# The norm's factor taken out of the opening's products: squares from x's own layout, products from a transposed x, a rescale at the end of the gates

## The chip, the cores and the metric

The kernel runs on one core of a Trainium2 chip. The metric is the time of one execution on the device in microseconds. Its engines are TensorE (PE, with its weight loads PEld), VectorE (DVE), ScalarE (ACT), GpSimd (POOL) and SyncE (SP), and each works through a queue of its own in order. Transfers are issued from the queues of SP, ACT and POOL.

## What is computed

One encoder layer for 512 tokens of width 2048, in float32. What matters here is its first step, a norm, and the projection behind it, of which the opening and the gates compute a part:

```python
def rmsnorm(x, w):
    y = x * lax.rsqrt(jnp.mean(x * x, axis=-1, keepdims=True) + EPS)
    return y * w

h = rmsnorm(x, norm_w)
u = h @ w_in        # columns: z_ssm, xbc, dt_f, dt_b, q_a, kv_a, z_attn, g_ssm, g_attn
xbc = silu(dwconv(xbc, conv_w, conv_b))          # along the tokens, 4 taps
dtf = softplus(dt_f + dt_bias_fwd)               # and dtb
y = ssd_scan(xs, dtf, ...) + flip(ssd_scan(...))
y = rmsnorm_groups(y * silu(z_ssm))
merged = sigmoid(g_ssm) * (y @ w_proj_ssm) + sigmoid(g_attn) * (o @ w_proj_attn)
return rmsnorm(x + merged @ w_out, final_norm_w)
```

The norm's factor is one number for each token, rsqrt(mean(x^2) + EPS), and h @ w_in is linear in it: it can be applied to h or to the product's rows.

## The kernel before

Every product in float32 is made of three products of rounded parts: a value is split into a high part (ScalarE casts) and the rest (VectorE subtracts), and high x high, high x low and low x high are added up in PSUM. `wchunk` (line 157) loads a chunk of 512 KB of a weight into `wraw`, casts it to `wh` and subtracts to `wl`, with three buffers for each; `mm3` (line 167) makes the three products. A tile of the projection has 16 such steps on 128 output columns and 512 tokens, from two chunks.

The opening (lines 195 to 241): x comes in eight transfers of 512 KB on SP's queue, in the layout tokens x width. ScalarE squares and sums each piece (line 210), `small_rsqrt` (lines 182 to 192) makes the factor of 128 tokens, VectorE and ScalarE scale x by it (lines 218 and 220), TensorE transposes it in 64 pieces (`x_turn`, line 225), and `x_out` (lines 227 to 230) makes h_h and h_l, the two parts of the transposed h, times the norm's weight. Then come the products: the tile of dt (`dtp`), and five tiles of xbc in the order 4, 5, 0, 1, 2, with a sixth, 3, after them. Each xbc tile goes through `conv_silu` (lines 384 to 393): a first step on ScalarE, three on VectorE, a SiLU on ScalarE, and is put to DRAM. After the second and the fourth of them `h_sums` (lines 706 to 731) makes, on half the width each, the sums that the Strassen products of the gates need: S1, S2 and S4 are split and kept, S3 and x21 are put to DRAM. `dt_make` (lines 278 to 303) turns dtp into dt and its decay in some twenty steps of VectorE, among the last xbc tiles.

Then the gates (lines 783 to 788): three weights of 2048 x 2048 (wz, wgs, wga), each in two pairs of columns by Strassen's scheme, a pair of seven products P1, P5, P6, P2, P3, P7 and P4 (`pair`, from line 642; `product`, line 545). A product has 48 steps of 128x512 and takes four chunks. X and Y are four buffers each: X is loaded for P1, then GpSimd adds the neighbouring block to it by a transfer that accumulates (`w_more`, line 497, issue on line 500), P5 takes that, VectorE adds Y for P6, and so on. In the first pair S3 is loaded back over a part of h_h (`h_part`), in the last pair of wga x21 (`h_back`). X, Y and the sums' buffers (pool `wx`) lie where the pool `sx` of the opening lay, and a buffer's first load waits for what last used the place. At a pair's end an activation (SiLU or sigmoid) is applied and the gate is put to DRAM. After the gates the state-space part begins: `dt_turn` (line 305) transposes dt, BT and CT and four xs are loaded from what the opening put (lines 897 to 901).

What sets the order: TensorE's order is the one in which the code is written. The other engines' instructions are ordered by a scheduler with priorities; `high_priority` with AHEAD = 60 or LOAD_AHEAD = 160 draws loads and splits forward.

## Time and profile before

| | us |
|---|---|
| time, median of 3 runs | 2056.31 (2055.39 to 2057.18) |
| the profiled execution | 2057.74 |
| its span, first to last instruction | 2055.9 |
| TensorE busy | 1967.2 (96%) |
| VectorE busy | 1463.4 (71%) |
| ScalarE busy | 968.9 (47%) |
| GpSimd busy | 317.7 (15%) |
| mean granted clock of TensorE | 0.986 |

The busy shares are means over the whole execution. The change touches the first 140 us, the last pair of wga and the head of the state-space part (from 571 us), so the timeline and windows of those places tell more than the page's shares. In a timeline a row is one instruction or a run of like ones, with what ended the idle time before it in brackets.

### The profile page before, as it was taken

Reading aid. Unit: us, or ns where it says so; the run is one execution under the profiler, and the core shown is the slowest. Engines: PE = TensorE matmul, PEld = TensorE weight load, DVE = VectorE, ACT = ScalarE, POOL = GpSimd, SP = SyncE. Lnnn points to the kernel's source line nnn. Section 1 sums busy time; section 2 is a strip of 40 time slices with the busy share of each in tenths; the row PEclk is TensorE's granted clock in tenths of the full one; section 3 lists DMA queues with packets and bytes.
Section 4 is the critical chain, followed back from the end, with each engine's and each line's share of the span. In section 5 each row is a group of like instructions: output and inputs, shape, how many; then the busy total and the mean of one; then the engine's idle time right before and its main releaser. Section 6 shows DMA issues by size and latency. Waiting matters only on the chain.

```text
span 2055.9 us, 24708 instructions
## 1 busy us (share of the span) xinstructions
PE 1967.2 (96%) x9074; PEld 1623.9 (79%) x9074; DVE 1463.4 (71%) x1946; ACT 968.9 (47%) x1352; POOL 317.7 (15%) x337
## 2 busy tenths in 40 slices
PE   6999999999989999998999989999999999999998
PEld 5878888888868787777788878888877777888886
DVE  7976676676659789799686567667675888776342
ACT  6444445444445656546545344444354454443232
POOL 0001011010033152332321101210010211100120
PEclk9999999999999999999999999999999999999999
DMA  5468657657446757687464857883386876865332
GB/s 196 164 179 202 171 126 195 184 120 188 134 169 188 220 149 209 201 231 220 150 194 149 232 164 185 221 209 88 83 212 246 302 256 260 273 219 169 108 118 82
DMA packets 166584, 378.56 MB, mean 184 GB/s; under 512 B 16000, under 2 KB 65280, under 8 KB 165888
## 3 DMA queue, kind: packets, MB, share of 16 engines
q1 hardware_dynamic: 104688, 238.33, 35.4%
q0 software_dynamic: 26944, 92.29, 20.5%
q10 hardware_dynamic: 34832, 46.38, 6.3%
q8 instruction: 71, 1.16, 0.2%
q14 instruction: 49, 0.40, 0.1%
HBM read 325.03 MB, written 98.04 MB: 206 GB/s over the span
## 4 chain that ended last, share of the span: by engine, by line
PE 72%; DVE 13%; DMA 7%; issue 4%; ACT 3%; SPq 0%; ACTq 0%; POOL 0%; DVEq 0%; POOLq 0%
PE P L564 10%; PE P L565 10%; PE P L563 10%; PE f L1497 3%; PE f L1498 3%; PE f L1496 3%; PE xbc L168 2%; PE xbc L169 2%; PE xbc L170 2%; PE za L168 2%; PE za L169 2%; DVE sum L1002 2%; PE za L170 2%; DVE wl L164 2%; DVE wl L434 1%
## 5 line engine op out<-in xcount | busy, mean ns | idle before, releaser
L434 DVE TENSOR_TENSOR wl<-X,wh 128x1024 fp32r<-128x1024 f32 x152 | 185.4, 1223 | 86.7 <-ACT wh L433 86.1
L164 DVE TENSOR_TENSOR wl<-wraw,wh 128x1024 fp32r<-128x1024 f32 (+2 forms) x148 | 171.9, 1162 | 89.7 <-ACT wh L163 89.4
L433 ACT CAST wh<-X 128x1024 fp32r<-128x1024 f32 x152 | 159.5, 1053 | 160.0 <-PE P L565 139.1
L163 ACT CAST wh<-wraw 128x1024 fp32r<-128x1024 f32 (+2 forms) x150 | 145.0, 969 | 147.5 <-PE za L169 41.9
L434 DVE TENSOR_TENSOR wl<-wraw,wh 128x1024 fp32r<-128x1024 f32 x74 | 91.4, 1235 | 97.5 <-ACT wh L433 97.4
L168 PE MATMUL xbc<-h_h,wh 128*128 128x512 f32 x384 | 151.9, 396 | 0.0
L170 PE MATMUL xbc<-h_h,wl 128*128 128x512 f32 x384 | 150.2, 391 | 0.9 <-DVE wl L164 0.9
L169 PE MATMUL xbc<-h_l,wh 128*128 128x512 f32 x384 | 149.9, 390 | 0.0
L563 PE MATMUL P<-wh,h_h 128*128 128x512 f32 x384 | 149.4, 389 | 0.0
L564 PE MATMUL P<-wl,h_h 128*128 128x512 f32 x384 | 149.4, 389 | 0.0
L565 PE MATMUL P<-wh,h_l 128*128 128x512 f32 x384 | 149.4, 389 | 0.0
L434 DVE TENSOR_TENSOR wl<-Y,wh 128x1024 fp32r<-128x1024 f32 x80 | 97.9, 1224 | 72.0 <-ACT wh L433 71.9
L433 ACT CAST wh<-wraw 128x1024 fp32r<-128x1024 f32 x74 | 78.0, 1054 | 144.7 <-PE f L1498 69.7
L433 ACT CAST wh<-Y 128x1024 fp32r<-128x1024 f32 x80 | 84.2, 1054 | 110.4 <-PE P L565 100.5
L564 PE MATMUL P<-wl,S 128*128 128x512 f32 x288 | 112.4, 390 | 0.8 <-DVE wl L434 0.8
L563 PE MATMUL P<-wh,S 128*128 128x512 f32 x288 | 112.1, 389 | 0.0
L565 PE MATMUL P<-wh,S 128*128 128x512 f32 x288 | 112.1, 389 | 0.0
L168 PE MATMUL za<-h_h,wh 128*128 128x512 f32 x256 | 101.7, 397 | 0.0
L170 PE MATMUL za<-h_h,wl 128*128 128x512 f32 x256 | 100.2, 391 | 1.0 <-DVE wl L164 1.0
L169 PE MATMUL za<-h_l,wh 128*128 128x512 f32 x256 | 100.0, 391 | 0.0
L1002 DVE TENSOR_TENSOR_SCAN sum<-da,scn 128x512 f32<-128x512 f32 x64 | 90.0, 1422 | 0.0
L170 PEld LDWEIGHTS xbc<-h_h,wl 128*128 128x128 f32 x384 | 72.4, 188 | 16.8 <-DVE wl L164 1.4
(634 smaller groups left out, 5184.6 us busy)
## 6 DMA issues: line engine op xcount, KB each, us to landing
wraw<-wi SPq DMA_DIRECT2D x102, 512.0 KB, 3.9
T_wps<-wps POOLq DMA_DIRECT2D x32, 512.0 KB, 6.0
da<-da_d SPq DMA_DIRECT2D x64, 256.0 KB, 4.5
T_wpa<-wpa POOLq DMA_DIRECT2D x32, 512.0 KB, 9.1
wraw<-wo SPq DMA_DIRECT2D x32, 512.0 KB, 3.4
wraw<-wps SPq DMA_DIRECT2D x24, 512.0 KB, 4.8
xbc_d<-xbc ACTq DMA_DIRECT2D x24, 256.0 KB, 3.7
wraw<-wun SPq DMA_DIRECT2D x16, 384.0 KB, 3.1
```

The lines of the kernel that those rows point to most:

```text
L163: act.copy(h, raw)
L164: (dve if ahead[0] else pool).tensor_sub(l, raw, h.bitcast(F32))
L168: pe.matmul(out, wh, xh, start=start, stop=False)
L169: pe.matmul(out, wh, xl, start=False, stop=False)
L170: pe.matmul(out, wl, xh, start=False, stop=stop)
L433: act.copy(hi_, raw)
L434: dve.tensor_sub(lo_, raw, hi_.bitcast(F32))
L563: pe.matmul(bs[i], xh, wh, start=(j == 0), stop=False)
L564: pe.matmul(bs[i], xh, wl, start=False, stop=False)
L565: pe.matmul(bs[i], xl, wh, start=False, stop=(j == 7))
L1002: dve.tensor_tensor_scan(sums[dd], flat(da), mask, 0.0, ALU.add, ALU.mult)
L1496: pe.matmul(acc, mh, wh, start=(start and k == 0), stop=False)
```

## The change

The host gives x a second time, transposed (`xt`), in pieces that lie as h_h does. h_h and h_l are made from it and the norm's weight, without the token's factor: no transposes, no scaling of x. The first three tiles (xbc 4, 5 and 0) are interleaved in the order "AAAABBBB AABB AABB C x 8, A x 8, B x 8, C x 8" as x's pieces land; two products on a constant stand ahead of them. x in its own layout is loaded after that, for the squares alone, through three buffers. `token_factors` makes the factor of all tokens at once, and `factor`, in TensorE's order at step 12 of the fourth xbc tile, spreads it to R (512 tokens in every partition) with four products; R is put to DRAM.

`xbc_done` multiplies a tile by R on VectorE ahead of its convolution, through one buffer `v_x`, for all six tiles. x_t is scaled by the norm's weight in place (16 operations of VectorE) and put to DRAM in eight pieces. `h_sums` takes x_t itself, so the eight additions of h_h and h_l go. dtp is the last tile; it is put to DRAM as it is, and `dt_make` runs in the first pair of wz, behind P5, from what it loads back, times R. The gates' activation takes the factor as its scale. In the last pair of wga, x11, x12, x21 and x22 are loaded back (eight transfers, before two), multiplied by R on VectorE and split over h_h and h_l, so that what comes after the gates has the norm's whole h. Lines of the Strassen class and of the head of wps are written differently with the same instructions.

The core of the diff:

```diff
-    act.dma_start(cst, a["cst"])
-    act.dma_start(vec, a["vec"])
+    act.dma_start(vec, a["vec"])
+    act.dma_start(cst, a["cst"])
...
+    warm_ps = pc("warm")
+    dve.memset(v_x, 1.0)
+    for _ in range(2):
+        pe.matmul(warm_ps, v_x[:, 0:P], v_x, start=True, stop=True)
+    ahead[0] = 1
+    firsts_i = (T_XBC + 4, T_XBC + 5, T_XBC)
+    early = [[] for _ in firsts_i]
+    for j in range(8):
+        for n, at in ((0, 0), (1, 2), (2, 4), (0, 4), (1, 6)):
+            if at == j:
+                early[n].append(wchunk(a["wi"][firsts_i[n], len(early[n])], 1024))
+        xs = x_t[:, 2 * j:2 * j + 2, :].rearrange("p k t -> p (k t)")
+        nc.sync.dma_start(xs, a["xt"][j])
+        for k in (2 * j, 2 * j + 1):
+            nw = vec[:, V_NORM + k:V_NORM + k + 1]
+            act.activation(h_h[:, k, :], x_t[:, k, :], AF.Copy, scale=nw)
+            dve.scalar_tensor_tensor(h_l[:, k, :], x_t[:, k, :], nw, h_h[:, k, :].bitcast(F32), ALU.mult, ALU.subtract)
+    early[2].append(wchunk(a["wi"][firsts_i[2], 1], 1024))
+    r4, ss = few(4), few(8)
     for t in range(TT):
...
+            xs = sxq("xs")
+            nc.sync.dma_start(xs, a["x"][t * P:(t + 1) * P, i * D // 2:(i + 1) * D // 2])
+            act.activation(xs, xs, AF.Square, accum_out=ss[:, 2 * t + i:2 * t + i + 1])
+        if t == 1:
+            fourth = [wchunk(a["wi"][T_XBC + 1, 0], 1024)]
...
+    def token_factors():
+        v4, rt = few(4), few(4)
+        sv = ss.rearrange("p (t i) -> p t i", i=2)
+        dve.tensor_add(v4, sv[:, :, 0], sv[:, :, 1])
+        dve.tensor_scalar(v4, v4, 1.0 / D, EPS, ALU.mult, ALU.add)
+        new = {"rt": rt, "rr": r4}
+        small_rsqrt(v4, 4, lambda n: new[n])
+        for t in range(TT):
+            dve.tensor_scalar_mul(v_x[:, t * P:(t + 1) * P], ident, r4[:, t:t + 1])
+    def factor():
+        rp = pc("rp")
+        for t in range(TT):
+            pe.matmul(rp[:, t * P:(t + 1) * P], ones, v_x[:, t * P:(t + 1) * P], start=True, stop=True)
+        act.copy(R, rp)
+        put(r_d, R)
...
+    def dt_make():
+        v, e = st("dv_"), st("e")[0:64, :]
+        u, pl = (sum_tile("pad") for _ in range(2))
+        nc.sync.dma_start(v, dv_d)
+        nc.sync.dma_start(u, r_d)
+        dve.tensor_mul(v, v, u)
...
     def h_sums(q):
-        def whole(name, i, j):
-            t = sxq(name)
-            h, l = part_of(i, j, q)
-            dve.tensor_add(view4(t), h.bitcast(F32), l.bitcast(F32))
-            return t
...
+        def x(i, j):
+            return x_t[:, 8 * j + 4 * q:8 * j + 4 * q + 4, i * 256:(i + 1) * 256]
...
+        s1, s3 = sxq("s1"), sxq("s3")
+        tc.keep_in_program_order(dve.tensor_sub(view4(s1), x(1, 0), x(1, 1)))
+        keep("S1", s1)
+        tc.keep_in_program_order(dve.tensor_sub(view4(s3), x(0, 0), x(1, 0)))
         put(h_d["S3"][:, cs], s3)
+        s2 = sxq("s2")
+        dve.tensor_sub(view4(s2), view4(s1), x(0, 0))
+        keep("S2", s2)
+        dve.tensor_add(view4(s1), view4(s2), x(0, 1))
+        keep("S4", s1)
...
+    def xbc_done(i, p_):
+        dve.tensor_mul(v_x, p_, R)
+        o = st("xbc")
+        put(xbc_d[0][i], conv_silu(v_x, (0, 1, 2, 3, 16, 20)[i], o, lambda n: o))
+    firsts = [mm("xbc") for _ in range(3)]
+    order = "AAAABBBB" + "AABB" * 2 + "C" * 8 + "A" * 8 + "B" * 8 + "C" * 8
+    for i in together([gemm_steps(p_, win(t), h_h, h_l, w_) for p_, t, w_ in zip(firsts, firsts_i, early)], order):
+        pass
+    ahead[0] = AHEAD
+    for k in range(KT):
+        tc.keep_in_program_order(dve.tensor_scalar_mul(x_t[:, k, :], x_t[:, k, :], vec[:, V_NORM + k:V_NORM + k + 1]))
+    for q in range(2):
+        for n, (j, i) in (("x11", (0, 0)), ("x12", (1, 0)), ("x21", (0, 1)), ("x22", (1, 1))):
+            put(view4(h_d[n][:, q * 1024:(q + 1) * 1024]), x_t[:, 8 * j + 4 * q:8 * j + 4 * q + 4, i * 256:(i + 1) * 256])
+    token_factors()
+    fourth_p = pb("xbc")
+    for i, _ in enumerate(gemm_steps(fourth_p, win(T_XBC + 1), h_h, h_l, fourth)):
+        if i == 12:
+            factor()
+    for i, p_ in zip((4, 5, 0, 1), firsts + [fourth_p]):
+        xbc_done(i, p_)
+    for i in (2, 3):
+        p_ = mm("xbc")
+        h_sums(i - 2)
+        run(gemm_steps(p_, win(T_XBC + i), h_h, h_l))
+        xbc_done(i, p_)
+    dtp = mm("dtp")
+    run(gemm_steps(dtp, win(T_DT), h_h, h_l))
...
-            act.activation(o, o, f)
+            act.activation(o, o, f, scale=r4[:, t:t + 1])
...
+    gates[2].hooks = {(1, "P1"): [r_load, h_load("x11"), h_scale("x11", 0), h_new("x11", 0, 0)],
+                      (1, "P2"): [h_load("x12"), h_scale("x12", 0), h_new("x12", 0, 1)],
+                      (1, "P3"): [h_load("x21"), h_scale("x21", 1)],
+                      (1, "P7"): [h_new("x21", 1, 0), h_load("x22", "Y"), h_scale("x22", 1)],
+                      (1, "P4"): [h_new("x22", 1, 1)]}
```

What moves on the queues, in the order in which the instructions stand. VectorE just before wz's first product (h_l is S3's low part, wl<-X the first chunks of wz), before the change:

```order
L292 SCALAR_TENSOR_TENSOR pl<-pl,u 64x512 x2
L293 SCALAR_TENSOR_TENSOR pl<-pl,e 64x512
L295 SCALAR_TENSOR_TENSOR dt_494<-pl,dv__493 64x512
L297 TENSOR_SCALAR da_891<-dt_494,small 64x512
L301 TENSOR_TENSOR pl<-dt_494,small 32x512
L389 SCALAR_TENSOR_TENSOR cacc<-xbc,vec,cacc 128x510
L390 SCALAR_TENSOR_TENSOR cacc<-xbc,vec,cacc 128x511
L391 SCALAR_TENSOR_TENSOR cacc<-xbc,vec,cacc 128x511
L434 TENSOR_TENSOR h_l<-xraw,h_h 128x4x256 x2
L434 TENSOR_TENSOR wl<-X,wh 128x1024 x2
```

The same place after the change (s_731 is S3 of the second half, S_239, S_240 and S_241 are S1, S2 and S4):

```order
L752 TENSOR_TENSOR v_x<-xbc,R 128x512
L737 TENSOR_TENSOR s_737<-s_730,x_t 128x1024
L442 TENSOR_TENSOR S_239<-s_730,S_239 128x1024
L734 TENSOR_TENSOR s_731<-x_t 128x1024
L442 TENSOR_TENSOR S_240<-s_737,S_240 128x1024
L739 TENSOR_TENSOR s_730<-s_737,x_t 128x1024
L398 SCALAR_TENSOR_TENSOR xbc<-v_x,vec,xbc 128x510
L399 SCALAR_TENSOR_TENSOR xbc<-v_x,vec,xbc 128x511
L442 TENSOR_TENSOR S_241<-s_730,S_241 128x1024
L400 SCALAR_TENSOR_TENSOR xbc<-v_x,vec,xbc 128x511
L442 TENSOR_TENSOR wl<-X,wh 128x1024 x5
```

The steps of dt_make have left this place, and the sums and splits of the second half, which stood well ahead of it, now stand right in front of wz's first wl.

SP's queue at the same place (X and Y are wz's blocks, xraw<-h_S the way back of S3, dt_4132 that of dt), before the change:

```order
L160 DMA wraw<-wi 128x1024 x14
L444 DMA xraw<-h_S_200 128x1024 x2
L464 DMA wraw<-wz 128x1024
L464 DMA X<-wz 128x1024 x4
L464 DMA Y<-wz 128x1024 x4
L464 DMA wraw<-wz 128x1024 x2
L779 DMA dt_4132<-dt_d 128x512
```

After the change (xs<-x are the pieces for the squares, dv and pad<-r_d what dt_make loads):

```order
L244 DMA xs<-x 128x1024 x4
L160 DMA wraw<-wi 128x1024 x7
L475 DMA X<-wz 128x1024 x4
L475 DMA Y<-wz 128x1024 x4
L819 DMA wraw<-h_S_202 128x1024 x2
L475 DMA wraw<-wz 128x1024
L283 DMA dv__1613<-dv_d 128x512
L284 DMA pad<-r_d 128x512
```

S3's way back has moved from ahead of X to behind Y, and dt_make's two loads have come in behind it.

SP's queue at the head of the state-space part (BT and CT are what it transposes first), before the change:

```order
L464 DMA wraw<-wga 128x1024
L160 DMA wraw<-wi 128x1024 x3
L769 DMA Y<-h_x_199 128x1024 x2
L160 DMA wraw<-wi 128x1024 x3
L897 DMA BT<-xbc_d_4_97 128x512
```

After the change:

```order
L819 DMA wraw<-h_x_199 128x1024 x2
L819 DMA wraw<-h_x_200 128x1024 x2
L160 DMA wraw<-wi 128x1024
L819 DMA Y<-h_x_201 128x1024 x2
L160 DMA wraw<-wi 128x1024 x4
L965 DMA BT<-xbc_d_4_97 128x512
```

Ahead of BT stand five loads of the next weights where there were six.

## Rows read from the trace of the kernel before

**Rows 1.** the page, its first part: an engine, its busy us, share and instructions.

```profile
PE 1967.2 (96%) x9074; PEld 1623.9 (79%) x9074; DVE 1463.4 (71%) x1946; ACT 968.9 (47%) x1352; POOL 317.7 (15%) x337
```

**Rows 2.** the timeline to 33 us: start, length, engine, line, operation, count, idle before.

```profile
7.58 1.06 ACT L210 ACTIVATE scr<-xt 128x1024 f32<-128x1024 f32 x1 [0.45 <-DMA xt<-x]
...
14.06 0.90 PE L225 MATMUL mm<-cst,xt 128*128 128x128 f32 x3 [0.94 <-DVE xt L220]
...
25.25 0.90 PE L225 MATMUL mm<-cst,xt 128*128 128x128 f32 x3 [6.30 <-DVE xt L220]
...
25.77 1.84 ACT L229 ACTIVATE h_h<-mm,vec 128x512 fp32r<-128x512 f32 x3
...
27.30 2.12 PE L225 MATMUL mm<-cst,xt 128*128 128x128 f32 x12
...
32.56 0.50 PE L168 MATMUL dtp<-h_h,wh 128*128 128x512 f32 x1
```

**Rows 3.** the transfers of the first 20 us, GB/s in 40 equal slices.

```profile
GB/s 0 0 0 66 135 250 279 268 289 295 400 394 412 423 414 370 410 426 426 426 410 418 426 426 418 410 426 418 434 410 410 426 434 418 410 393 123 0 0 0
```

**Rows 4.** the timeline of TensorE: P1 of wz begins; two waits in its P5.

```profile
108.87 0.39 PE L563 MATMUL P<-wh,h_h 128*128 128x512 f32 x1
...
123.41 0.50 PE L564 MATMUL P<-wl,S 128*128 128x512 f32 x1 [0.47 <-DVE wl L434]
...
126.75 0.50 PE L564 MATMUL P<-wl,S 128*128 128x512 f32 x1 [0.34 <-DVE wl L434]
```

**Rows 5.** windows: stretch and length, then busy time of PE, PEld, DVE, ACT, POOL.

```profile
10.00:20.00 10.00, 5.91 (x24) 4.71 (x24) 6.75 (x25) 8.96 (x18) 0.63 (x1) 1.00 0.83 340
...
120.00:140.00 20.00, 19.19 (x82) 14.89 (x82) 17.39 (x15) 10.36 (x12) 0.00 (x0) 1.00 0.32 71
140.00:160.00 20.00, 20.00 (x90) 16.57 (x89) 13.55 (x15) 8.62 (x10) 2.88 (x4) 1.00 0.68 176
```

**Rows 6.** the timeline of VectorE from 58 us on.

```profile
66.59 1.21 DVE L710 TENSOR_TENSOR x<-h_h,h_l 128x1024 f32<-128x1024 f32 x1
67.72 0.73 DVE L389 SCALAR_TENSOR_TENSOR cacc<-xbc,vec,cacc 128x510 f32<-128x510 f32 x1
68.38 1.20 DVE L164 TENSOR_TENSOR wl<-wraw,wh 128x1024 fp32r<-128x1024 f32 x1
...
76.04 3.33 DVE L287 RECIPROCAL u<-u 64x512 f32<-64x512 f32 x1
```

**Rows 7.** groups by line (mean ns) and transfers (us to landing), before 140 us.

```profile
L433 ACT CAST wh<-X 128x1024 fp32r<-128x1024 f32 x12 | 12.4, 1050 | 12.3 <-DMA X<-wz 9.9 <-PE P L565 2.4
...
L388 ACT ACTIVATE cacc<-xbc,vec 128x512 f32<-128x512 f32 x5 | 3.9, 773 | 4.1 <-PE xbc L170 4.1
...
L292 DVE SCALAR_TENSOR_TENSOR pl<-pl,u 64x512 f32<-64x512 f32 x8 | 5.4, 678 | 0.1
...
wraw<-wi SPq DMA_DIRECT2D x14, 512.0 KB, 3.6
...
h_S<-s ACTq DMA_DIRECT2D x2, 512.0 KB, 4.2
```

**Rows 8.** line 500, GpSimd's additions to X of wz, 95 to 135 us.

```profile
L500 POOL DMA_DIRECT2D X<-wz x4: 854/868/1037, 107.4 to 114.4; - x4
...
DMA to landing us min/median/max: 10.0/12.2/12.9
```

**Rows 9.** a window: the last pair of wga, columns as in rows 5.

```profile
491.00:568.00 77.00, 77.00 (x341) 63.81 (x340) 54.96 (x55) 37.91 (x43) 6.05 (x7) 1.00 0.51 129
```

**Rows 10.** timeline and a window (with PEclk) of the state-space head, from 564 us.

```profile
564.71 5.77 SPq L160 DMA_DIRECT2D wraw<-wi  x3
570.57 0.43 SPq L897 DMA_DIRECT2D BT<-xbc_d  x1
...
576.80 0.63 PE L879 MATMUL pb<-cst,BT 128*128 128x128 f32 x4 [2.86 <-DMA BT<-xbc_d]
...
568.00:592.00 24.00, 16.09 (x71) 12.79 (x71) 6.68 (x8) 10.35 (x17) 7.33 (x7) 0.79 0.50 175
```

More of the change, by code (lines that the diff above doesn't have):

```diff
@@ L197, in build @@
     h_l = hp.tile([P, KT, SEQ], F32R, name="h_l")
-    xp = open_pool("xp", side="right")
+    so = open_pool("so", side="right", reuse_waits="tile")
+    s_op = {w: so.tile([P, 2, 8, 256], F32R, name=w) for w in ("S1", "S2", "S4")}
+    xp = open_pool("xp", side="right", reuse_waits="tile")
+    sx = open_pool("sx", reuse_waits="tile")
+    x_t = xp.tile([P, KT, SEQ], F32, name="x_t")
     warm = few(1)
@@ L577, in __init__ @@
             self.ahead = {}
+            self.spare = "ms" if self.made else "u"
         def hook(self, cp, name):
@@ L627, in head, with head_end @@
             self.p1 = (a, b)
[L628 removed]
+        def head_end(self):
+            return self.second(1, self.p1[1], lambda i: sum_tile("p5"), None, "P2b")
         def pair(self, cp, headed=False):
@@ new lines, in h_load, with f, h_scale @@
+    def h_load(which, tag="w", in_order=False):
+        def f():
+            h_ops.raws[which] = []
+            for q in range(2):
+                t = w_tile(tag)
+                made = nc.sync.dma_start(t, h_d[which][:, q * 1024:(q + 1) * 1024])
+                if in_order:
+                    tc.keep_in_program_order(made)
+                h_ops.raws[which].append(t)
+        return f
+    def h_scale(which, i):
+        def f():
+            for t in h_ops.raws[which]:
+                dve.tensor_mul(view4(t), view4(t), r_back[0][:, i * 256:(i + 1) * 256].unsqueeze(1).broadcast_to([P, 4, 256]))
+        return f
@@ L785, in build @@
+    gates[0].first_columns(0)
+    first_pair = gates[0].pair(0)
+    for _ in range(8):
+        next(first_pair)
+    dv_ = st("dv_")
+    tc.keep_in_program_order(act.copy(dv_, dtp))
+    put(dv_d, dv_)
+    run(first_pair)
+    run(gates[0].pair(1))
+    for p_ in gates[1:]:
         for cp in range(2):
```

172 lines of the change are left out of this document (61 added, 111 removed).

## Prediction

> **What bounds the kernel now.** I read the page first: TensorE is busy 1967.2 us, 96% of the span [rows 1], so a change counts only where TensorE waits, or where it makes TensorE wait. Then I read the opening as a timeline: squares as x lands, the last transposes behind a wait of 6.30 us for the scaled x at 25.25, and the first product only at 32.56 [rows 2]. From there seven tiles of products follow one another until P1 of wz starts at 108.87 [rows 4]: 76.3 us, 10.9 a tile. Windows show what the other engines have left: VectorE has 2.6 of 20 us free from 120 to 140 and 6.5 from 140 to 160 [rows 5]. So the opening's wait is on the path, but VectorE has almost no room behind it.
>
> **Part 1, the start.** The transposes, their copies and the wait for the factor go. The first two 512 KB transfers are what is needed (a weight chunk and a piece of x): in the trace of before the second piece was there at 7.58; with its cast (three took 1.84 us) the first product starts at 8.3 [rows 2]. That is 24.3 us earlier. Two things take from it. The four small products that spread the factor are under 0.6 us (from the 12 transposes in 2.12 us). And TensorE's clock: three transposes took 0.90 us at 14.06, twelve took 2.12 us at 27.30 [rows 2], so the first ran at the lower of its two levels (1.2 and 2.4 GHz) and it rose about 28. Ends: nothing lost if it rises at once; (28.4 - 8.3) / 2 = 10.1 us if it rises where it did before. [...] TensorE alone would then reach P1 at 8.3 + 76.3 + 0.6 + 3 = 88.2, 20.7 us earlier than before.
>
> **Part 2, when the factor R is there.** Its four products stand in TensorE's queue at step 12 of the fourth tile: 8.3 + 3 + 3.75 x 10.9 = 52.2, with the copy 53.4. The other side is ScalarE: casts use three buffers, so the fourth waits until 14 steps of 0.68 us have run, 8.3 + 3 + 9.5 = 20.8; then three casts (1.05 [rows 7]), seven h_h (0.6) and eight squares (1.06 each) are some 16 us, up to 6 more as the last five loads of x wait for a square to free one of three buffers, and the square root stands behind eight puts (0.43 an issue [rows 10], 3.4): 40 to 47. The transfers themselves are no limit: 23 of 512 KB at 420 GB/s [rows 3], 1.25 us each, end at 35. So TensorE's place decides, with some 5 us to spare.
>
> **Part 3, VectorE from R to X.** The convolutions need R, and the sums, which don't, stand behind them in VectorE's queue. Up to the second half's S3 VectorE has in its queue 6 products by R, 15 convolution steps and 15 operations on 1024 columns (four wl, eleven of the sums and splits). In [rows 6] an operation on 1024 columns is followed after 1.13 us and a convolution step after 0.66, their own lengths are 1.21 and 0.73; so 3.9 + 9.9 to 11.0 + 17.0 to 18.2, that is 30.8 to 33.1. Four times it also waits for ScalarE's first step of the convolution (0.77 us [rows 7], with the hand-over I put 1.1): 4.4. S3 is made at 53.4 + 36.4 = 89.8 (88.6 to 90.9). X for wz lies where these buffers lay, so its load waits for the put of S3 (4.2 us) and takes 3.6 itself [rows 7]; a cast, 1.05: P1 starts at 98.6. TensorE stands idle from 88.2, over 10 us; of the 20.7, 10.3 are left.
>
> **Part 4, P5.** P5 needs X + Y's neighbour added by GpSimd's transfers, each issued after wl of its chunk. Before, X had been loaded before P1, and the four were issued from 107.4 to 114.4 and landed 10.0 to 12.9 us later [rows 8]: 117.4 to 127.3, 3.3 us apart; P5 waited 0.8 us in all [rows 4]. Now the first is issued at 98.6 + 1.2 and lands at 109.8. The spacing is 3.3 us as before, or wider, since X, Y and S3 now come in the same stretch (11 transfers of 1.25 us among four additions make it up to 4.7). I take 4, nearer to the row: the last lands at 121.8, and with a cast and a quarter of a product (2.7) P5 ends at 125.6 (123.5 to 127.7). Without that wait it would end near 121.5.
>
> **Part 5, dt_make.** It moves from the opening to behind P5: 8 steps of 0.68, a reciprocal of 3.33 and nine smaller, about 14 us on VectorE [rows 6, 7], where 9.1 us are free in 120 to 160 [rows 5]. In VectorE's order the reciprocal stands right ahead of two wl of P6. Ends: nothing, and 6 us (what does not fit); I take 3. P2 starts at 125.6 + 10.9 + 3 = 139.5. Before it was 108.87 + 3 x 10.9 and 0.8 of waits: 142.4. Of 24.3 us at the start, 2.9 are left.
>
> **Part 6, the last pair of wga.** Six more loads of 512 KB, eight products by R and six more splits: 14 x 1.21 = 16.9 us on VectorE, which is busy 54.96 of 77 us there [rows 9]. It fits with 5 us to spare; ends 0 and 5, I take 0.5. The scale in the gates' last activation costs nothing that a row shows, as it takes the place of the same instruction without it.
>
> **Part 7, the head of the state-space part.** Before BT stood a weight load more on SP's queue; three such loads were issued over 5.77 us, and TensorE then waited 2.86 us for BT [rows 10]. With one load fewer, BT goes out some 2.7 us earlier: that wait goes, 2.9. Ends: 0 (if ScalarE's table load and exponentials, which come next, just take its place) and 5 (if the stretch at the lower clock, 24 us at a mean of 0.79 [rows 10], shrinks as well).
>
> **Sum:** -2.9 + 0.5 - 2.9 = -5.3. Against the profiled execution's own 2057.7 (span 2055.9) that is 2052.4; it stood 1.4 above the median of 2056.3, so 2051.0 for the median. With the ends of parts 4 to 7 the forecast's own range is 2046 to 2056. What a measurement of this kernel can tell from no change is 0.2%, 4 us: faster is below 2052.2, slower above 2060.4.
>
> **Rival: the clock.** If TensorE stays at the lower level until 28 as before, 10.1 us are lost and not 3; R, S3, P1 and P6 all come 7.1 us later, and the time is 2058. For it: before, its work in bits did not raise the clock before 28 [rows 2]; against: those were transposes between waits, and now products queue. After idle stretches the level fell again later: 24 us at a mean of 0.79 behind the waits at 576 [rows 10] is 10 us at the lower level. The Trainium skill (TensorE: Matmul & The Clock Gate, "HAM oscillation — how this bites in real kernels") says that waits for data between bursts put the array back to its slow clock, and that each burst then starts slow; the rows agree for 576. By the same rule P1, after an idle 10 us, would lose 5 us. Worked out here, that is mostly no loss: P1 would end at 115.5 rather than 110.5, and P5's last quarter waits for its addition until 122.9 anyway, so under 1 us.
>
> **Rival, slower: the additions.** If the four transfers of part 4 come over 7 us apart instead of 4, P5 ends 9 us later or more and all is given back with a loss: at 7.5 us, 2051.0 + 3 x 3.5 = 2061.5. Below a spacing of 7.0 it is not slower. For it: each took 10 to 12.9 us from issue to landing, and more loads run beside them now, with dt_make's VectorE work ahead of the operations that free buffers. Against: four Y loads and two weight loads ran beside them before as well, at 3.3.
>
> **Rival: the plain gain.** If X can be loaded as early as TensorE wants it (VectorE's queue is shorter than I think, or the buffers are free sooner), P1 starts at 88.2 and nothing is waited for: 2056.3 - 20.7 - 2.9 = 2032.7. Against it stand 31 us of VectorE work behind an R that TensorE itself sets.
>
> **How the numbers follow.** Forecast 0.58, clock 0.16, additions 0.17, plain gain 0.09. Of the forecast's range 2046 to 2056 some six tenths lie below 2052.2: faster 0.36 + 0.09 = 0.45; same 0.22 + 0.16 = 0.38; slower 0.17. The range leaves out the plain gain and the far end of the additions: 2045 to 2062.
>
> **What would show it.** Part 1: first product near 8.3, and the rise of the clock seen in the spacing of the first products. Part 2: R's copy near 53. Part 3: a wait of TensorE of about 10 us before P1, ended by the load or cast of X, P1 near 98.6. Part 4: waits of ScalarE's casts for X in P5, 5 us in all on TensorE. Part 5: P2 near 139.5. Part 6: no wait of TensorE over 0.5 us in the last pair of wga. Part 7: no wait for BT. A P1 near 88 or past 104 would make parts 2 or 3 wrong; a wait in wga's last pair, part 6.

## The result and the profile after

The changed kernel is slower: 2067.86 us median (2061.19 to 2071.33) against 2057.18 (2055.39 to 2061.12) for the kernel before, ratio 1.0040 with a 95% interval of 1.0025 to 1.0055; on another chip the two gave 1.0045 (1.0025 to 1.0065). The forecast was 2051.0, with 2045 to 2062 as its range. The profiled execution took 2068.28, its span is 2066.5, 10.6 more than before.

TensorE's first product does start 25 us earlier, and nothing of that is left by P2 of wz. The steps of the prediction beside the trace of after (start times in us; the kernel before in the last column):

| step | predicted | after | before |
|---|---|---|---|
| first product | 8.3 | 7.48 | 32.56 |
| R copied out of PSUM (end) | 53.4 | 55.76 | |
| S3 of the second half made | 89.8 | 93.77 | |
| P1 of wz | 98.6 | 101.57 | 108.87 |
| P6 (end of P5) | 125.6 | 129.60 | 132.41 |
| P2 | 139.5 | 144.09 | 143.29 |
| added by the last pair of wga | 0.5 | 6.5 | |
| taken away at the head of the state-space part (BT) | 2.9 | 2.9 | |

To follow a lead or a delay beyond that, I count TensorE's instructions from the end of both programs (their order is the same from the gates' end on) and compare their starts. From P2 on the changed kernel is 0.8 us late, after the last pair of wga 7.3, in the head of the state-space part (577 us) 4.4, at 1480 us 0.9, and at the end 10.5.

ScalarE in the opening of after (start, length, engine, line, operation, idle before and what ended it; ACTq is its issue of transfers):

```profile
44.96 7.35 ACTq L214 DMA_DIRECT2D h_x<-x_t  x6
52.35 0.21 ACT L185 ACTIVATE small<-small 128x4 f32<-128x4 f32 x1 [6.36 <-DMA h_x<-x_t]
...
55.17 0.59 ACT L265 COPY R<-rp 128x512 f32<-128x512 f32 x1 [0.73 <-PE rp L264]
```

The six puts of h's quarters that stood ahead of the square root held ScalarE from 46 to 52.35: 7.35 us from the first issue to the end of the last, not the 0.43 each of [rows 10]. The row is a chain and not one cost. Two of the six were issued at once, and then none until 48.81; the same timeline from 46.2 us on begins with the other four:

```profile
48.81 3.50 ACTq L214 DMA_DIRECT2D h_x<-x_t  x4
```

The third of the six waited 2.7 us there, for the first of the eight puts to land: that one was issued at 37.73, landed at 48.8, and both use one signal. The issues themselves took 0.37 to 1.25 us each. A put took a median of 7.8 us to land:

```profile
h_x<-x_t ACTq DMA_DIRECT2D x8, 512.0 KB, 7.8
```

The path from S3 to P1, in the timeline of after, and two windows (stretch, its length, busy time of PE, PEld, DVE, ACT, POOL, then the granted clock of TensorE and the transfers' share):

```profile
92.55 1.22 DVE L734 TENSOR_TENSOR s<-x_t 128x1024 f32<-128x1024 f32 x1
...
93.80 0.33 ACTq L214 DMA_DIRECT2D h_S<-s  x1
...
96.46 3.49 SPq L475 DMA_DIRECT2D X<-wz  x4
...
99.38 0.63 ACT L401 ACTIVATE xbc<-xbc 128x512 f32<-128x512 f32 x1 [2.26 <-DVE xbc L400]
...
100.47 1.04 ACT L442 CAST wh<-X 128x1024 fp32r<-128x1024 f32 x1 [0.47 <-ACT xbc L401]
...
101.57 0.79 PE L574 MATMUL P<-wh,h_h 128*128 128x512 f32 x1 [11.18 <-ACT wh L442]
```

```profile
90.00:100.00 10.00, 0.39 (x2) 0.00 (x0) 9.25 (x10) 4.24 (x5) 0.00 (x0) 0.68 0.37 136
100.00:110.00 10.00, 7.96 (x23) 6.02 (x24) 4.86 (x4) 4.67 (x6) 2.75 (x3) 0.63 0.98 330
```

In the first window TensorE works 0.39 of 10 us while VectorE works 9.25: that is the wait of 11.18. Two chains end there almost together: X's first chunk landed at 99.7, and the sixth tile's SiLU (line 401), which stands ahead of its cast on ScalarE, ended at 100.01. The clock falls to the lower level (1.2 GHz) at 93.7, in the wait, and is back at 107.3, so P1's first product takes 0.79 us where [rows 4] has 0.39.

The end of the gates in after: TensorE's wait, then the two waits of VectorE that lead to it.

```profile
556.36 0.79 PE L575 MATMUL P<-wl,h_h 128*128 128x512 f32 x1 [3.85 <-DVE wl L442]
```

```profile
548.84 0.69 DVE L608 TENSOR_TENSOR p<-p,P 128x512 f32<-128x512 f32 x1 [1.41 <-DMA ga_d<-p]
...
553.35 0.69 DVE L608 TENSOR_TENSOR p<-p,P 128x512 f32<-128x512 f32 x1 [3.82 <-DMA ga_d<-p]
```

The puts of ga_d for which VectorE waits, us from issue to landing, first in after (538 to 540 us), then in before (536 to 548):

```profile
DMA to landing us min/median/max: 9.9/12.0/14.1
```

```profile
DMA to landing us min/median/max: 3.8/4.1/4.3
```

The window from 545 to 568 us, first of after, then of before:

```profile
545.00:568.00 23.00, 19.15 (x75) 15.27 (x74) 14.88 (x16) 11.30 (x13) 0.00 (x0) 0.85 0.54 161
```

```profile
545.00:568.00 23.00, 23.00 (x103) 19.07 (x102) 16.72 (x19) 12.57 (x15) 0.00 (x0) 1.00 0.38 128
```

The kernel before worked without a gap there (23.00 of 23). After idles 3.85 and its clock is at the lower level from 554.5 to 561.3: the wait and half of the 4.9 us that it works at that level are 6.3, the 6.5 of the table but for 0.2. The wait for BT of [rows 10] is gone, as predicted; TensorE waits in the head for ScalarE's exponentials, as in before (3.63):

```profile
585.46 1.11 PE L947 MATMUL pb<-cst,xs 128*128 128x128 f32 x4 [3.68 <-ACT dec L331]
```

The last loss is in a stage whose instructions are the same. From 1480 to 1760 us TensorE works 264.59 of 280 us in before (first row) and 257.44 in after:

```profile
1480.00:1760.00 280.00, 264.59 (x1150) 213.54 (x1149) 219.02 (x268) 136.58 (x169) 34.91 (x56) 0.97 0.75 248
```

```profile
1480.00:1760.00 280.00, 257.44 (x1118) 206.92 (x1117) 212.72 (x261) 133.86 (x168) 33.68 (x54) 0.97 0.75 241
```

### The profile page after: what moved, and what is told of

Read it like the earlier page. It is cut to its first block, busy times and chain, and to the rows that moved or that the text cites. A ratio compares the mean times of both kernels' runs of the same rounds, so it can differ in the third digit from the quotient of the medians.

```text
span 2066.5 us, 24676 instructions
## 1 busy us (share of the span) xinstructions
PE 1968.8 (95%) x9022; PEld 1621.6 (78%) x9022; DVE 1471.5 (71%) x1955; ACT 977.5 (47%) x1354; POOL 313.1 (15%) x335
## 4 chain that ended last, share of the span: by engine, by line
PE 69%; DVE 13%; DMA 10%; ACT 4%; issue 3%; ACTq 0%; SPq 0%; DVEq 0%
PE P L575 9%; PE P L576 9%; PE P L574 9%; PE f L1569 3%; PE f L1570 3%; PE f L1568 3%; DMA wraw<-wps 2%; PE za L168 2%; PE za L169 2%; PE za L170 2%; DVE wl L164 2%; DVE sum L1070 2%; PE xbc L169 2%; PE xbc L168 2%; PE xbc L170 2%
## 5 line engine op out<-in xcount | busy, mean ns | idle before, releaser
L163 ACT CAST wh<-wraw 128x1024 fp32r<-128x1024 f32 (+2 forms) x150 | 144.7, 967 | 125.6 <-PE za L169 42.1
L574 PE MATMUL P<-wh,h_h 128*128 128x512 f32 x384 | 151.4, 394 | 11.2 <-ACT wh L442 11.2
L442 DVE TENSOR_TENSOR wl<-wraw,wh 128x1024 fp32r<-128x1024 f32 x74 | 91.3, 1235 | 98.8 <-ACT wh L442 98.7
L574 PEld LDWEIGHTS P<-wh,h_h 128*128 128x128 f32 x384 | 73.2, 191 | 27.1 <-ACT wh L442 11.6
L575 PEld LDWEIGHTS P<-wl,h_h 128*128 128x128 f32 x384 | 73.2, 191 | 20.5 <-DVE wl L442 5.2
```

What stands on the lines that cost most here:

```text
L163: act.copy(h, raw)
L442: made = act.copy(hi_, raw), dve.tensor_sub(lo_, raw, hi_.bitcast(F32))
L574: pe.matmul(bs[i], xh, wh, start=(j == 0), stop=False)
L575: pe.matmul(bs[i], xh, wl, start=False, stop=False)
```

## Experiments

Times are medians; the ratio is to the kernel before on the same chip. "Idle" is TensorE's.

### Do both traces repeat?

The two kernels again, unchanged.

> The kernel before, unchanged, for a second profile. Theory (the stage from 1480 us to the end, where both kernels have the same instructions in the same order, differs from execution to execution by its waits for transfers and by where the clock falls): idle time of TensorE from 1480 us to the end differs from the first profile's 15.7 us by 2 us or more. Rival (that stage is steady and the change itself makes it slower): 15 to 17 us again.

> The changed kernel, unchanged, for a second profile. Up to 600 us both theories expect the same as in the first: P1 of wz near 101.6, TensorE idle 11 us before it, some 4 us of wait in the last pair of wga. From 1480 us on, theory (chance of the execution): TensorE's idle time differs from the first profile's 24.9 us by 2 us or more. Rival (the change makes that stage slower): 24 to 26 us again.

before_again took 2055.9, after_again 2066.76 (ratio 1.0045, 1.0025 to 1.0065). P1 of wz started at 102.22 behind a wait of 11.2, the wait near 557 was 4.2, and between 1480 and 1760 the two idled 16.8 and 22.9 us. All three losses repeat.

### The opening: what makes P1 wait

**sums_early** puts the sums of h ahead of R in the program:

```diff
     token_factors()
+    h_sums(0)
+    h_sums(1)
     fourth_p = pb("xbc")
...
         p_ = mm("xbc")
-        h_sums(i - 2)
```

> The sums for the Strassen products stand ahead of the products by R in the program, nothing else is changed. Theory (P1 of wz waits for VectorE's queue: the sums stand behind the convolutions, and X lies where their buffers lay): S3 is made some 20 us earlier, X is loaded while dtp still runs, TensorE's wait of 11.2 us before P1 falls to under 4, P1 starts at 92 to 97, the clock does not fall there, and the time is 3 to 8 us under the changed kernel's. Rival (P1 waits for R and for the transfers themselves): P1 stays at 100 to 103 and the time within 2 us of the changed kernel's.

2065.2 (ratio 1.0049, 1.0034 to 1.0064), not to be told from the changed kernel. TensorE's waits from 30 to 145 us (engine, line waited for, us in total, times, longest):

```profile
PE xbc L168 <- ACT wh L163: 4.9, 1, 4.9
PE P L575 <- DVE wl L442: 4.9, 5, 2.1
PE xbc L168 <- DVE v_x L752: 4.1, 2, 3.8
PE P L574 <- ACT wh L442: 2.7, 1, 2.7
```

The wait ahead of P1 fell from 11.2 to 2.7, but P1 started at 105.72. New waits of 8.8 us came before it: 4.9 inside the fourth tile, for a cast of its weights that now stood behind the puts on ScalarE, and 3.8 ahead of the fifth, for the first product by R, which now stood behind six operations of the sums on VectorE (59.31 to 66.25). Behind each of them the clock fell (51.8 to 58.7 and 65.5 to 72.3). Only the place of the wait changed.

**puts_late** writes h's puts behind the fourth tile's product:

```diff
-    for q in range(2):
-        for n, (j, i) in (("x11", (0, 0)), ("x12", (1, 0)), ("x21", (0, 1)), ("x22", (1, 1))):
...
     token_factors()
...
+    for q in range(2):
+        for n, (j, i) in (("x11", (0, 0)), ("x12", (1, 0)), ("x21", (0, 1)), ("x22", (1, 1))):
...
     for i, p_ in zip((4, 5, 0, 1), firsts + [fourth_p]):
```

> The eight puts of h's quarters (x11, x12, x21, x22) are written behind the fourth tile's product instead of ahead of it, so that the square root of the token factors stands on ScalarE ahead of seven of them. Theory (the puts held the square root, and through it R, by 6 us): square root at 46 to 47.5 us instead of 52.35, R ready 53.4 or earlier with TensorE's wait of 2.59 us at 54.0 gone, S3 1.5 to 3 us sooner; but ScalarE must issue the puts among the casts later, so P1 comes 0 to 3 us sooner (98.5 to 101.5) and the time falls by 0 to 3 us. Rival (R's time doesn't matter, the queue behind it is set by ScalarE's casts and the fourth to seventh tiles' weights): R comes sooner, P1 stays at 101 to 103 us, and the time stays within 1 us.

2062.41 (2056.13 to 2066.38), ratio 1.0020 (1.0006 to 1.0034). The timeline of ScalarE:

```profile
45.70 0.20 ACT L185 ACTIVATE small<-small 128x4 f32<-128x4 f32 x1
...
52.41 0.59 ACT L265 COPY R<-rp 128x512 f32<-128x512 f32 x1 [4.98 <-PE rp L264]
```

The square root came 6.65 us sooner; R, now set by TensorE's place, 2.76 sooner; TensorE's wait of 2.59 at 54 was gone; P1 started at 98.79 and P2 at 140.87, 3.2 sooner than in after. The theory holds; the puts had set R. P1 still waited 11.7.

**v2_rebalanced** puts the first half's sums ahead of R and the second half's behind the second tile, the puts late, gives the last four tiles' weights a higher priority, keeps dt_make's loads in order, and gives the third gate's sum a tile of its own (sum_in_pad, below).

> Four repairs at once: the sums of h of the first half ahead of R and of the second half behind the second of the six tiles, weights of the last four tiles at a higher priority, puts of h behind the fourth product, the two loads of dt_make kept in their order so that dt_make stays ahead of P6, and the sum tile of the third gate in a tile of its own. Theory (each wait found, 11.2 us before P1, 2.59 at 54, 2.1 before P6, is a queue behind one wrong place and comes off): P1 at 90 to 95 us with a wait under 4 us, no clock fall over 7 us before 145 us, P2 3 to 8 us sooner than in the changed kernel, time 2056 to 2062. Rival (the opening has more work on VectorE and ScalarE than TensorE's products cover, so that any order moves the wait): the idle time of TensorE between 30 and 145 us stays at 15 us or more, and the time at 2063 to 2068.

2059.58 (2053.8 to 2069.29), ratio 1.0019 (1.0001 to 1.0037). For the opening the rival holds: P1 at 102.32 with 15.4 us of idle time from 30 to 145 (6.0 for the product by R at 60, 7.5 ahead of P1). Its time lies in the theory's range all the same: dt_make's wait of 2.1 in P6 is gone, and the wait at the gates' end was 3.0.

So the sums and puts could be moved and P1 stayed between 98.8 and 105.7. In two of these runs X itself was no longer late: in sums_early its first chunk was asked for at 77.80 us, 18.7 sooner than in after, and landed at 81.0; its first cast still came at 104.63, behind the sixth tile's SiLU (in v2_rebalanced 83.10 and 101.23):

```profile
77.80 26.12 SPq L475 DMA_DIRECT2D X<-wz  x4
...
104.63 1.99 ACT L442 CAST wh<-X 128x1024 fp32r<-128x1024 f32 x2 [0.45 <-ACT xbc L401]
```

Two things thus stand ahead of P1. X lies in the place of the buffers through which S3 and R pass, so that in after its load waited for the last of VectorE's queue; and its splits stand behind the last taps, which holds P1 where X comes early. **open_only** changes both (X and Y in the place of x_t, the taps of the last three tiles behind P1's splits) and takes over puts_late (contrary to its expectation dt_make's loads are not pinned in it; its reciprocal fell behind P6 by itself, at 140.99):

```diff
-    x_t = xp.tile([P, KT, SEQ], F32, name="x_t")
+    x_q = [xp.tile([P, 4, SEQ], F32, name=f"x_t{q}") for q in range(4)]
...
+    sums_at = {4: 0, 0: 1}
+    for i, p_ in zip((4, 5, 0, 1), firsts + [fourth_p]):
...
+        if i in sums_at:
+            h_sums(sums_at[i])
...
+    cols = open_pool("wy", side="right", reuse_waits="tile")
+    for tag in ("Y", "X"):
...
+    for _ in range(4):
+        next(first_pair)
+    xbc_conv(1, True)
```

> The changed kernel with its opening put in another order and place, the rescale at the gates' end as it is: x_t is four tiles of 8 KB instead of one of 32; the weights X of the first gate's P1 lie in the half of x_t that the sums S1 and S3 read last but that no later step reads, instead of in the place of the tiles that S3 and R pass through; the sums stand behind the first and the third of the six tiles, the taps of the last three tiles behind P1's first splits, the puts of h behind the fourth product, dt_make's loads in program order. Theory (P1 waits for VectorE's queue only because its memory and its splits stand behind that queue): TensorE goes from the last product of the opening at about 87 us into P1 with a wait of 0 to 4 us, P1 at 87 to 92 us instead of 101.6, clock whole from 30 to 145 us or under 7 us of half, P5 no later than 16 us behind P1, P2 10 us or more sooner than in the changed kernel; time 2047 to 2056. Rival (additions and casts hold P5 where it was, so the lead is given back): P5 waits 8 us or more in sum, P2 within 4 us of the changed kernel, time 2060 or more.

2050.48 (2046.85 to 2055.46), ratio 0.9980 (0.9968 to 0.9993), faster than the kernel before. TensorE's timeline, and a window as above:

```profile
89.10 0.50 PE L581 MATMUL P<-wh,h_h 128*128 128x512 f32 x1 [1.23 <-ACT wh L449]
...
90.67 0.50 PE L582 MATMUL P<-wl,h_h 128*128 128x512 f32 x1 [1.06 <-DVE wl L449]
```

```profile
90.00:100.00 10.00, 9.33 (x34) 7.54 (x35) 8.17 (x10) 4.38 (x5) 3.61 (x4) 0.83 1.04 333
```

P1 started at 89.10 instead of 101.57, with waits of 1.23 and 1.06; the clock was at its lower level for 3.4 us, not 13.7; P2 started at 130.28, 13.8 sooner. VectorE's work is the same and still fills 80 to 90 us (9.97 of 10); it is only no longer between TensorE and P1. The run changes memory and order together, so it doesn't tell how much each gave; the two runs above show that an early X alone doesn't move P1. Of the 13.0 us by which its P2 leads the kernel before, 8 are left at the end: 5.7 go in the last pair of wga, where TensorE waits 3.7 us (3.85 in after).

### The last pair of wga

**sum_in_pad** gives the third gate's sum a tile that the put of the one before doesn't hold:

```diff
-                o = sum_tile(self.spare if headed else "p1")
+                o = sum_tile(self.spare if headed else "pad" if self.w == "wga" else "p1")
```

> In wga the sum behind P3 goes into a buffer that no transfer reads, not into the one whose put is on its way; nothing else is changed. Theory (in the last pair VectorE stands for 1.4 and 3.8 us behind the puts of the gate, and the low part of P7's weight behind it is late): the two waits go, TensorE's wait of 3.85 us near 556 us goes with the fall of the clock after it, 5 to 7 us less. Rival (VectorE has too much work there, with eight products by R and six more splits): VectorE has no wait but the low part is late all the same, TensorE still waits over 2 us there and the time is within 2 us of the changed kernel's.

2064.92 (ratio 1.0048, 1.0032 to 1.0064), not to be told from the changed kernel. VectorE's waits for ga_d were gone; in their place, from 540 to 565 us:

```profile
PE P L575 <- DVE wl L442: 3.1, 1, 3.1
```

```profile
DVE Y L829 <- DMA Y<-h_x: 4.7, 1, 4.7
```

Now it waited for the reload of x22. Not one put was slow, but all the transfers there: the two puts took 9.9 and 14.1 us to land, the four additions to Y a median of 9.2 against 6.3 in before.

**no_reload** leaves the rescale out (only the reload of x21 stays):

```diff
-    gates[2].hooks = {(1, "P1"): [r_load, h_load("x11"), h_scale("x11", 0), h_new("x11", 0, 0)],
...
+    gates[2].hooks = {(1, "P7"): [h_load("x21", "Y"), h_new("x21", 1, 0)]}
```

> The changed kernel without the rescale of h at the end of the gates: of the reloads of h only the one of x21 that the kernel before has too is left, so the loads, multiplications by R and new splits of the other three quarters of h are left out of the computation. Theory (the reloads jam the transfers and stop the last pair of the third gate product): the waits of 3.1 to 4.2 us of TensorE near 557 us fall under 1 us, and the clock doesn't fall between 150 and 570 us; time 4 to 8 us below the changed kernel, ratio to the kernel before 1.001 to 1.003. Rival (the waits there come from additions and puts that the kernel before has as well, shifted by the lead): a wait of 3 us or more stays, and the time falls by less than 2 us.

2061.2 (ratio 1.0021, 1.0004 to 1.0039). The median is 5.6 below that of after_again, on another chip; the intervals overlap, so the times alone don't show the gain. The trace does: no wait of TensorE and no fall of the clock between 145 and 570 us, and TensorE is 0.5 us behind the kernel before at 570 us as it was at P2. The theory holds. **rescale_in_place** does the whole rescale, without those loads:

```diff
+    def h_sum(which, i, j, tag="w"):
...
+                dve.tensor_add(view4(t), h.bitcast(F32), l.bitcast(F32))
...
-    gates[2].hooks = {(1, "P1"): [r_load, h_load("x11"), h_scale("x11", 0), h_new("x11", 0, 0)],
+    gates[2].hooks = {(1, "P1"): [r_load, h_sum("x11", 0, 0), h_scale("x11", 0), h_new("x11", 0, 0)],
```

> The changed kernel with h's quarters x11, x12 and x22 made again from their own halves at the gates' end (VectorE adds h_h and h_l, multiplies by R, and the sum is split again), so that of the reloads only that of x21 and of R is left; the puts in the opening stay. VectorE gets six more 128x1024 additions there, 1.2 us each. Theory (the transfers, not the arithmetic, make the waits near 557 us): TensorE's waits there fall under 1 us, no clock fall between 145 and 570 us, offset at 575 us 4 to 6 us below the changed kernel's, time 2059 to 2064, as with the rescale left out (2061.2). Rival (VectorE's work in the last pair is the bound): waits of 2 us or more stay, time within 2 us of the changed kernel.

2069.27 (ratio 1.0069, 1.0044 to 1.0093): the waits at 557 us fell to 0.4 as expected, the puts of ga_d there landed in 4.5 to 4.8 us, and the time did not fall (its interval overlaps the changed kernel's). The expectation missed what comes next. SyncE's timeline, and TensorE's waits from 540 to 592 us:

```profile
545.37 32.40 SPq L160 DMA_DIRECT2D wraw<-wi  x6
577.86 0.38 SPq L975 DMA_DIRECT2D BT<-xbc_d  x1
```

```profile
PE pb L957 <- DMA BT<-xbc_d: 4.8, 1, 4.8
PE pb L957 <- ACT dec L331: 2.3, 1, 2.3
PE pa L327 <- ACT daT L321: 2.0, 1, 2.0
```

The raw halves sit in the buffers of the next stage's weights while VectorE works on them, so six weight loads wait at the head of SyncE's queue, and the load of BT behind them: the wait for BT is back, 4.8 us where [rows 10] has 2.86, and others behind it. (Its P1 was 2.6 later than in after as well, at 104.16; the opening is the same.) **rescale_bt_first** pins the loads of BT, CT and the four xs behind the first of those six, and makes x22's raw halves in the third and fourth tile of Y:

```diff
+        given = None if g else [wchunk(a["wi"][T_XBC + 6, 0], 1024)]
...
+            if g == 0:
+                tc.keep_in_program_order(made[0])
...
+            with tc.issue_after(made[-1].ins):
+                gap()
```

> The changed kernel's opening; rescale in place as in rescale_in_place (2069.3 us, with waits of 9.8 us and 10.2 us of half clock between 570 and 600 us), and BT's, CT's and the xs' loads behind one weight chunk instead of six. Theory (SyncE's queue took back the gain): idle time there under 4 us, time 2054 to 2062. Rival (something else than the queue holds that stage): idle time there 7 us or more, time 2066 or more.

2062.72 (ratio 1.0028, 1.0016 to 1.0041), a median 6.6 less. In the traces TensorE is 5.3 us earlier at 600 us than in rescale_in_place, but 2.0 of that stand at P2 already, in an opening that is the same; about 3 us came in the head of the state-space part, where BT's wait is gone. How much of the 6.6 the queue gave is thus not shown. TensorE still idled 7.4 us in the head (9.8 before), 4.7 of it for ScalarE's copies of the transposed xs, which the theory had at under 4 in all, and the time is just above its range.

### Both together

**v11_both** is open_only with rescale_in_place, dt_make's loads in order and only x21's puts; **best** adds rescale_bt_first's order of loads.

> The new opening and the rescale in place together; of h's puts only x21's two are left. If the two repairs add up: P1 at 87 to 92 us, P2 15 us or more sooner than in the changed kernel, no wait over 1 us near 557 us, and a time of 2040 to 2050, below the kernel before (2055.6). If the lead is given back on the way (at P5's additions, or at the gates' end by VectorE): 2053 to 2060.

> The new opening, the rescale in place, and the loads of BT, CT and the four xs of the first state group on SyncE's queue behind the first weight chunk of the products that fill the waits, instead of behind six; x22's raw halves in the third and fourth Y tile, so that CT's memory is free sooner. Theory (what the rescale gained at 557 us was lost in SyncE's queue ahead of BT): TensorE's idle time from the gates' end to the first state product falls from 9.0 us to under 3, half clock there from 13.7 us to under 4, time 2034 to 2043. Rival (the weights of the filling products then come late instead): new waits of 4 us or more in that stage, time within 3 us of 2047.8.

v11_both: 2047.79 (2041.81 to 2050.63), ratio 0.9957 (0.9939 to 0.9975), with P1 at 86.68, P2 at 127.25 and a wait of 0.3 near 557: the two repairs add up. best: 2040.74 (2037.87 to 2048.08), ratio 0.9925 (0.9899 to 0.9950), 17 us below the kernel before. Both beat both kernels. In best P1 starts at 86.65 and P2 at 126.70, 17.4 sooner than in after. TensorE's waits in best, 540 to 592 us:

```profile
PE pb L1004 <- ACT xT L1015: 6.8, 2, 6.2
PE pa L328 <- ACT daT L322: 2.6, 1, 2.6
PE pb L1004 <- ACT dec L332: 0.8, 1, 0.8
```

That is 10.2 us against 8.8 in v11_both, where 3.3 were for BT: the wait moved on to the transposed xs. New waits of over 4 us are what best's rival expected, but from late weights; these are for ScalarE's copies. The traces of the two differ by 1.5 us in span, and their intervals overlap, so that BT's order gains on top of the new opening is not shown. A wait of 5.3 ahead of P5 (for the copy of dtp) is left as well.

### The stage after 1480 us

The three runs that move scratch tensors in memory each change one number in one line, as here before_shift (448 in after_4mb, 1600 in best_shift):

```diff
-    kr_d = dr.tile([64, SEQ], F32, name="kr_d")
+    kr_d = dr.tile([1728, SEQ], F32, name="kr_d")[0:64]
```

> The kernel before, with one scratch tensor (kr_d) made longer by 3,407,872 bytes, which moves every scratch tensor behind it in memory to the place that it has in the changed kernel; no instruction moves on any engine. After 1480 us the order of instructions is the same in both kernels, and still TensorE idled 15.7 and 17.0 us there in two runs of the kernel before, and 22.2 to 24.9 us in four runs of the changed kernel and its variants. Theory (the place of the scratch in memory makes late transfers slower): idle time of TensorE after 1480 us 21 us or more, and a time 4 to 9 us over the kernel before. Rival (what is left over from the gates, h's own values in another rounding or another offset of the engines against each other, makes it): idle time under 18.5 us, and a time within 2 us of the kernel before.

> The changed kernel with one scratch tensor (kr_d) made longer, so that the scratch tensors of the later stages lie 4,194,304 bytes behind their place in the kernel before instead of 3,407,872. No instruction moves. Theory (the place modulo some power of two sets the speed of late transfers): TensorE's idle time after 1480 us falls from 22.2 to 24.9 us to under 18.5, time 3 to 6 us below the changed kernel. Rival (place is not it): 21 us or more, time within 2 us of the changed kernel.

> The kernel before, profiled a third time. If the stage after 1480 us is steady: TensorE idle there 15 to 18 us, as in the two profiles so far (15.7, 17.0). If it is the spread of single profiles: 20 us or more.

> The changed kernel, profiled a third time, on the same chip. If the loss after 1480 us is steady: TensorE idle there 22 to 25 us, as in the two profiles so far (24.9, 24.3), and 5 us or more above the kernel before. If it is the spread of single profiles: under 20 us, or within 3 us of the kernel before.

> The kernel best with kr_d made longer by 3,145,728 bytes, so that the later stages' scratch tensors lie where they lie in the changed kernel (3,407,872 bytes behind those of the kernel before). If the place makes the loss after 1480 us: TensorE idle there 20 us or more (15.5 in best), time 4 to 8 us above best (2040.7). If not: idle under 18 us, time within 3 us of best.

The expectations count the idle time to the end of the span; the table takes 1480 to 1760 us alone (280 less the busy time of PE).

| kernel | late scratch behind its place in before | idle, us | time, us |
|---|---|---|---|
| before, three profiles | 0 | 15.4, 16.8, 15.7 | 2055.6 to 2057.9 |
| before_shift | 3.25 MB | 16.6 | 2058.31, ratio 1.0009 (0.9992 to 1.0026) |
| after, three profiles | 3.25 MB | 22.6, 22.9, 20.5 | 2063.7 to 2067.9 |
| after_4mb | 4 MB | 18.6 | 2062.07, ratio 1.0037 (1.0023 to 1.0052) |
| v11_both, best | 0.25 MB | 16.0, 15.5 | 2047.79, 2040.74 |
| best_shift | 3.25 MB | 21.4 | 2046.34, ratio 0.9955 (0.9940 to 0.9970) |

```profile
1480.00:1760.00 280.00, 264.49 (x1152) 213.57 (x1151) 219.68 (x260) 136.83 (x163) 34.58 (x59) 0.98 0.76 254
```

```profile
1480.00:1760.00 280.00, 258.65 (x1118) 207.83 (x1117) 214.28 (x253) 133.50 (x158) 33.05 (x55) 0.97 0.75 249
```

The two rows are best and best_shift: the same instructions, scratch 3 MB further on, 5.8 us less work done in the stage and 5.6 us more time. In this pair the idle time goes with the place, by more than three profiles of after differ among themselves (2.4 us). The times don't show it: the intervals of the two ratios overlap (0.9899 to 0.9950 and 0.9940 to 0.9970). In the kernel before the place changed nothing: before_shift idled 16.6, where 21 to the end was expected (18.0 measured). And after_4mb idled 20.2 us to the end, between its theory (under 18.5) and its rival (21 or more). All other variants of the changed kernel lie at 3.25 MB, between 17.9 (no_reload) and 22.7 (rescale_bt_first).

So every profile of a changed kernel with its scratch 3.25 MB on idled 17.9 us or more there, and every profile at the place of before, or 0.25 MB from it, under 17. But the size of the loss is no steady number: from 1480 us to the end the three pairs of traces give 9.6, 10.9 and 1.5 us, and the third pair met neither expectation (idle to the end 20.8 beside 17.6). I take from it that the place of the scratch may be a part of the loss in the changed kernel: one pair of profiles speaks for it, before_shift against, and it is not shown. What makes a place good, why before_shift did not lose, and how much of the 9.6 is the spread of single executions stays open.

## Why the prediction was wrong

**Part 1** held: first product 7.48 (8.3), and the clock, at the upper level (2.4 GHz) for the first product, was at the lower from 8.4 to 11.8, which costs some 2 us and not the 3 taken or the rival's 10.1. That 3 us would be lost no row or run shows.

**Part 2** failed, in a term that it held to be covered. It saw that the square root stands behind eight puts and charged them 0.43 each, "some 5 us to spare". That is the price of a single issue. The six behind one another took 7.35 us, 2.7 of them a wait for an earlier put to land, the spare was gone, and R ended at 55.76 instead of 53.4. puts_late shows it: with the puts behind, R is where the part had put it (52.41 to 53.0).

**Part 3** was right in its mechanism and nearly in size: from R's end to S3 38.0 us (36.4), from S3 to P1 7.8 (8.8). Late by part 2's 2.4 and this, P1 came at 101.57, 3.0 late. open_only shows that the mechanism is memory and splits behind VectorE's queue; the part named the memory alone, and sums_early and v2_rebalanced show that the splits' place by itself holds P1 as late. The rival of the plain gain (P1 at 88.2) is what a kernel without it does (89.10, 86.65).

**Part 4** held: P1 to the end of P5 took 28.0 us, 27.0 predicted, in another split. P1 took 14.2 instead of 10.9, since it ran at the lower clock until 107.3, and P5 waited 2.0 us in all where 5 were named. The Trainium skill (TensorE: Matmul & The Clock Gate, "HAM oscillation — how this bites in real kernels") says that a wait for data puts TensorE back to its slow clock and that the next burst starts slow; the rows at 90 to 110 us agree (lower level from 93.7 to 107.3). That this would cost under 1 us, as P5 waits for its additions anyway, was about right. The additions landed 3.7 to 3.9 us apart, 4 in the prediction, and not the 7 of its rival.

**Part 5**: P6 took 14.5 us, 13.9 predicted. With the 3.0 of parts 2 and 3, the 1.0 of part 4 and this 0.6, P2 came 4.6 later than predicted: 0.8 late instead of 2.9 early, as P2 of the kernel before stood at 143.29 and not at the 142.4 of the sum.

**Part 6** is the largest step that failed: 0.5 taken, 5 as its far end, 6.5 measured. It priced the six reloads by VectorE's 16.9 us of work and held them to fit; their transfers it left out. The runs show the opposite: in rescale_in_place VectorE has the same work and six additions more, the loads are gone, the puts of ga_d land in 4.5 to 4.8 us, and the waits fall to 0.4. That transfers from every queue share the same engines is in the Trainium skill (DMA: Bandwidth & Descriptors, "Issuing engines are not separate DMA queues"); the trace agrees: the puts of ga_d took 9.9 and 14.1 us to land beside the reloads and four additions, 3.8 to 4.3 in before.

**Part 7** held (2.9): BT's load was issued at 575.16 with TensorE 7.3 us late, that is 2.7 earlier against TensorE than the 570.57 of [rows 10]. It held in a kernel whose last pair is late. In the runs without that delay the wait for BT or its neighbours is back (7.7 us of idle in no_reload, 9.8 in rescale_in_place, 7.4 in rescale_bt_first). Each of them also changes what stands in SyncE's queue, so that parts 6 and 7 hang together is likely, but not shown.

**What was left out**: the sum took all behind the head to be unchanged. In the profiled pair it gained 3.5 us between 575 and 1480 and lost 9.6 from there to the end, in stages whose instructions are the same; the change also moved their scratch tensors, since it added others ahead of them, and that may be a part of the loss; its cause stays open. From the sum of -5.3 to the measured 10.5 there are 15.8: 3.7 by P2, 6.0 in wga's last pair, nothing at BT, -3.5 and 9.6 behind.

## What to carry to other kernels

When work is taken off the start of the longest queue, ask where the memory of the next stage's first operand lies and who reads that memory last, and what stands ahead of that operand's casts on their engines: P1 waited for a buffer's last reader and, where X came early, for its casts' turn. A new place for both was worth more than any order of the sums. Price a move through memory as a transfer beside all others in flight, not only by the engine that issues it or works on it; data still on the chip may be cheaper to make again. And when a wait is removed, look at the head of the next queue that it fed (here SyncE's, with BT behind six weight loads) before counting the gain.

## What the runs showed of the hardware

Issues of transfers can hold their engine for longer than their own price: six puts of 512 KB from ScalarE, in runs of 1 KB (256 columns of 4 bytes), held it for 7.35 us, and the instruction behind them waited 6.36. Their issues took 0.37 to 1.25 us each, where two that stood alone took 0.38 and 0.40, and 2.7 us were a wait for an earlier put to land. A 256 KB put took 9.9 to 14.1 us to land beside reloads and additions, 4.5 to 4.8 without six of the reloads (rescale_in_place) and 3.8 to 4.3 in before. Whether the place of scratch tensors in memory changes a late stage is not shown: with it 3 MB further on, TensorE idled 5.8 us more there in one kernel, and nothing that can be told in another.
